# Re-ordering the steps of VectorE, ScalarE, GpSimd and the transfers of a hybrid attention layer, with TensorE's order and every address kept

## The chip, the core and the metric

The kernel runs on one core of a Trainium2 chip. TensorE (PE) does the matrix products into PSUM, which has eight banks; VectorE (DVE), ScalarE (ACT) and GpSimd (POOL) work beside it, and nearly all transfers are issued from SyncE's queue (SP). Each engine executes its own instructions strictly in the order in which they were written; engines wait for one another by semaphores. The metric is the device time of one execution in microseconds (us).

## What is computed

One decoder layer on a sequence of 512 rows of width 1024, in float32. The reference, cut to its skeleton:

```python
h = rms_norm(x, attn_pre_norm[l])
mix = hybrid_mixer(h, ...)          # one input projection, two head groups, one output projection
x = x + rms_norm(mix, attn_post_norm[l])
h = rms_norm(x, ffn_pre_norm[l])
f = (silu(h @ w_gate[l]) * (h @ w_up[l])) @ w_down[l]
x = x + rms_norm(f, ffn_post_norm[l])
```

The mixer has a differential attention of 4 heads (steps whose names begin with D) and a sparse attention of 8 heads with compressed, selected and sliding-window branches (steps that begin with N). With 512 rows every block is selected, so the selected and the window branch come down to causal attention.

## The kernel before

**Precision.** A float32 operand is cut into a high part (a rounding copy, on ScalarE mostly) and a low part (the difference, on VectorE mostly). A product is then three fast TensorE products: high by high, low by high, high by low. That is why almost every TensorE step has a ScalarE step and a VectorE step ahead of it.

**Stages in time, by the profile.** Up to about 140 us: input projection (`F`), compression and rotation of heads. From 140 to 245 us: the attention heads, with scores, row maxima (`L1051`, DVE), exponentials (`L1055`, ACT), multiplication by gates and row sums (`L1224`, POOL), transposes (`L1072`, PE), cutting of the transposed parts (`L1082` on ACT, `L1085` on DVE) and the products with the values. From 245 to 295: output projection, norms, transposes. From 295 to 505: the gate and up products of the feed-forward part, written as a seven-product scheme of 2x2 blocks (`block`, L1582). For each of 22 column blocks f there are two weight loads (`load_ff`), differences of weights (`sum_ff`, DVE), the high parts (`high_ff`, ACT) and low parts (`low_ff`, DVE at L1576), seven products of 12 matmuls each, and the evacuation of PSUM: `snap_1` and `snap_2` (ACT) copy a bank between two products, `sum_x` (DVE, L1610) and `sums` (DVE, L1626) add, `gate_x` and `gate_c` (ACT) apply silu, `mult` (DVE, L1632) multiplies. From 500 to 586: the down product in a similar scheme, with loads `load_d` and `load_22`, weight differences `sums_a` (DVE, L1682 to L1688), low parts `low_d` (L1720), `left_a` (L1699) and `right_a` (L1708), and products `product_a`, `product_b` (L1665); then the last columns (`down`, L1814) and the final norm and rows (`last_sum` to `last_row`, L1836 to L1871).

**What sets the order.** The builder defines named steps (`op`, `at`) and then calls them in the order of three lists: `PLAN` for everything up to the output projection, `PLAN_NORM` for the norms and the feed-forward part, and `PLAN_END` for its end; steps of the feed-forward part in neither of the last two lists stand between them by a planner's due time (the first argument of `at`). A step issues its instructions on its engine when it is called. So the order of the names in the lists is the order of the work on each engine and on SP's queue. A step such as `pair_sums.6.4` issues a VectorE instruction and also one or two spills to DRAM from SP's queue.

**Memory.** Every tile has a fixed place. Tags with several buffers (`raw`, `hi`, `lo`, the eight PSUM banks `b`, and others) rotate in the order of the calls; the wide buffers of the two big pools are given by tables of letters (`S_HOMES`, `HOMES`). A step that writes a place must wait until the last reader of the place's earlier tile is done: `block.18.4` accumulates into a PSUM bank that `sums.18` has to read first; `load_d.2` overwrites the weights that `low_d.0` reads; `load_22.1` those that `sums_a.0.0` and `sums_a.0.2` read. Two engines that use one PSUM bank are kept apart as well.

Of the kernel before, what the change touches and what calls it, by code (L numbers as in the profile page):

```python
# [46 lines left out]
wu xL1 gc bL1.0 xH1 xl1 bL1.1 bh1.0 F0.0.1 bl1.0 F0.1.1 F0.2.1 bh1.1 bl1.1 F2.0.1 bL1.2 bh1.2 F2.1.1 bl1.2 F2.2.1  # L47
F1.0.1 F1.1.1 F1.2.1 xS1 bL2.0 F4.0.1 F4.2.1 bh2.0 bl2.0 F4.1.1 F3.0.1 F5.2.1 F3.1.1 F3.2.1 F5.0.1 F5.1.1 xL2 xH2
F4.0.2 bL3.0 F2.0.2 F0.0.2 F0.1.2 xl2 F1.0.2 F5.1.2 bh3.0 bl3.0 xL3 xH3 F2.1.2 F2.2.2 F5.0.2 F3.0.2 F0.2.2 xl3
F1.1.2 F4.0.3 F5.2.2 F4.1.2 F3.1.2 F0.0.3 F4.2.2 xL0 xS2 xH0 F4.1.3 F3.2.2 xl0 F5.2.3 F5.0.3 F1.2.2 F5.1.3 F1.0.3  # L50
F1.1.3 F1.2.3 xS3 xA3 bL0.0 bh0.0 bl0.0 F5.2.0 F4.0.0 F4.2.3 F5.0.0 F2.0.3 xS0 F1.0.0 xL4 xH4 xl4 F2.1.3 F2.2.3
bL4.0 bh4.0 xA2 F0.1.3 F0.2.3 F5.2.4 F2.0.0 F2.1.0 F2.2.0 bl4.0 F5.1.4 xL7 xH7 F5.1.0 F0.0.0 F0.1.0 xL5 xH5 xS4 xl7
xS7 xl5 xS5 F3.0.3 cL F4.1.4 F3.1.3 F3.2.3 F3.0.0 F3.1.0 F3.2.0 F5.0.4 xL6 xH6 bL5.0 cc lL bh5.0 xl6 xA4 F1.1.0 Lv00
F4.2.4 F2.0.4 F2.1.4 F4.2.0 F4.2.5 F3.0.4 F3.1.4 xA5 F1.2.0 F3.2.4 F1.0.4 F1.1.4 xS6 xA6 F5.2.5 xA7 xA1 F0.2.0 bl5.0
# [2092 lines left out]
```

## Time and profile before

| | |
|---|---|
| median of 3 runs | 622.14 us (621.75 to 622.27) |
| the profiled execution | 622.45 us, of which its span is 620.5 us |
| moved by transfers | 98.41 MB, mean 159 GB/s |

The profile shows one execution. "Busy" is the time in which an engine had at least one instruction at work; matmuls are pipelined, so a busy TensorE may still start its matmuls more slowly than it could. Behind a row in square brackets stands how long the engine was idle before it, and whose signal ended that. "PEclk" is the TensorE clock that was granted, as a share of full speed.

### The profile page before, as it was taken

How to read it: one execution, taken by the hardware profiler on the slowest of the kernel's cores; microseconds unless marked ns; L12 is line 12 of the kernel's file. 1: busy time of each engine (PE TensorE's matmuls, PEld its weight loads, DVE VectorE, ACT ScalarE, POOL GpSimd, SP SyncE). 2: the span in 40 equal slices, each digit the busy share in tenths (PEclk: the TensorE clock that was granted, in tenths of full speed). 3: DMA queues.
4: the chain of work that ended last, by engine and by line, in shares of the span. 5: the costliest groups of instructions: out<-in, count | busy, mean ns of one | idle time of the engine just before them, and what ended most of it. 6: DMA issues, size and time to landing. Idle time of an engine off the chain costs nothing. (4 is left out here: it accounts for less than half of the span.)

```text
span 620.5 us, 10992 instructions
## 1 busy us (share of the span) xinstructions
PE 607.1 (98%) x4065; PEld 549.9 (89%) x4065; DVE 546.4 (88%) x965; ACT 373.9 (60%) x784; POOL 101.4 (16%) x153
## 2 busy tenths in 40 slices
PE   9999999999999999999999999999999799999995
PEld 5888888899999988889999999999999788878884
DVE  5898898997898884999999998899999699899977
ACT  6445375467999986577584565446464365577522
POOL 0030000307868878100000000000000000000000
PEclk9999999999999999999999999999999989999998
DMA  8566986646233211545143434353531554677413
GB/s 263 187 224 248 299 296 230 216 146 248 101 119 101 88 34 63 182 165 203 59 146 104 156 117 136 119 178 121 175 102 54 174 165 140 201 222 252 135 41 130
DMA packets 38341, 98.41 MB, mean 159 GB/s; under 512 B 4240, under 2 KB 11792, under 8 KB 37392
## 3 DMA queue, kind: packets, MB, share of 16 engines
q1 hardware_dynamic: 38144, 97.59, 47.3%
q8 instruction: 32, 0.52, 0.3%
q14 instruction: 21, 0.17, 0.1%
q10 hardware_dynamic: 144, 0.13, 0.1%
HBM read 82.10 MB, written 15.60 MB: 157 GB/s over the span
## 5 line engine op out<-in xcount | busy, mean ns | idle before, releaser
L1867 POOL TENSOR_TENSOR uf<-c,gain 128x512 f32<-128x512 f32 x1 | 1.3, 1277 | 360.1 <-DVE c L1836 360.1
L1055 ACT ACTIVATE p<-sc,nm 128x512 f32<-128x512 f32 (+3 forms) x96 | 50.2, 530 | 14.4 <-DVE nm L1051 12.9
L1051 DVE TENSOR_REDUCE nm<-sc 128x1 f32<-128x384 f32 (+3 forms) x96 | 43.4, 483 | 8.6 <-PE sc L1047 5.5
L1591 PE MATMUL yz<-rope,wbh 128*128 128x256 f32 x352 | 48.0, 280 | 0.0
L1224 POOL TENSOR_TENSOR p<-p,l 128x256 f32<-128x256 f32 (+3 forms) x64 | 45.3, 732 | 1.0
L1591 PEld LDWEIGHTS yz<-rope,wbh 128*128 128x128 f32 x352 | 44.1, 191 | 0.1
L1085 DVE TENSOR_TENSOR ptl<-tr,pth 128x384 fp32r<-128x384 f32 (+1 forms) x60 | 34.3, 592 | 8.4 <-ACT pth L1082 8.4
L1082 ACT ACTIVATE pth<-tr 128x384 fp32r<-128x384 f32 (+1 forms) x60 | 29.9, 530 | 7.3 <-PE tr L1072 6.8
L1568 ACT ACTIVATE whi<-wraw 128x1024 fp32r<-128x1024 f32 x22 | 23.2, 1057 | 13.3 <-DMA wraw<-in_wg 12.5
L1568 ACT ACTIVATE wbh<-wraw 128x1024 fp32r<-128x1024 f32 x22 | 23.3, 1057 | 12.6 <-DVE wraw L1555 7.7
L1576 DVE TENSOR_TENSOR wel<-e,weh 128x1024 fp32r<-128x1024 f32 x22 | 26.7, 1219 | 3.9 <-ACT weh L1568 2.6
L1568 ACT ACTIVATE weh<-e 128x1024 fp32r<-128x1024 f32 x22 | 23.2, 1056 | 8.0 <-DVE e L1550 6.9
L1072 PE MATMUL tr<-ident,p 128*128 128x128 f32 x200 | 27.8, 274 | 0.0
L1714 ACT ACTIVATE whi<-wraw 128x1024 fp32r<-128x1024 f32 x20 | 21.0, 1057 | 10.9 <-PE acc L1665 5.7
L1591 PE MATMUL yz<-rope,wbl 128*128 128x256 f32 x176 | 27.2, 276 | 0.0
L1576 DVE TENSOR_TENSOR wlo<-wraw,whi 128x1024 fp32r<-128x1024 f32 x22 | 26.8, 1217 | 0.0
L1576 DVE TENSOR_TENSOR wbl<-wraw,wbh 128x1024 fp32r<-128x1024 f32 x22 | 26.7, 1217 | 0.0
L1720 DVE TENSOR_TENSOR wlo<-wraw,whi 128x1024 fp32r<-128x1024 f32 x20 | 24.1, 1218 | 1.1 <-ACT whi L1714 1.1
L1621 ACT ACTIVATE us<-yz 128x512 f32<-128x512 f32 x22 | 13.0, 592 | 18.7 <-PE yz L1591 15.7
L1591 PEld LDWEIGHTS yz<-rope,wbl 128*128 128x128 f32 x176 | 23.4, 188 | 0.0
L1041 PE MATMUL sc<-kst,qst 128*128 128x384 f32 (+3 forms) x64 | 23.0, 367 | 0.3 <-DMA kst<-qk 0.3
L1072 PEld LDWEIGHTS tr<-ident,p 128*128 128x128 f32 x200 | 22.4, 141 | 0.7
(382 smaller groups left out, 1993.9 us busy)
## 6 DMA issues: line engine op xcount, KB each, us to landing
wraw<-in_wg SPq DMA_DIRECT2D x24, 512.0 KB, 3.7
wraw<-in_wu SPq DMA_DIRECT2D x22, 512.0 KB, 3.4
wraw<-in_wd SPq DMA_DIRECT2D x22, 512.0 KB, 3.7
qk<-rope SPq DMA_DIRECT2D x7, 1024.0 KB, 5.9
kst<-qk SPq DMA_DIRECT2D x24, 256.0 KB, 4.2
wraw<-in_wf SPq DMA_DIRECT2D x10, 512.0 KB, 4.2
wraw<-in_wo SPq DMA_DIRECT2D x8, 512.0 KB, 4.4
qst<-qk SPq DMA_DIRECT2D x16, 256.0 KB, 2.7
```

Source lines behind the costliest of these rows:

```text
L1041: pe.matmul(sv[i], lhs, kk[:, 0, :w], start=(n == 0), stop=False, skip_group_check=True)
L1051: dve.tensor_reduce(nm[i], sv[i], AX.X, OP.max, negate=True)
L1055: act.activation(pp[i], sv[i], AF.Exp, bias=nm[i], accum_out=hs["l"][:, row, i:i + 1])
L1072: pe.transpose(tr[:, n * P:(n + 1) * P], pp[i][:, j * P:(j + 1) * P], ident)
L1082: act.activation(part(u, 0), tv[u], AF.Copy)
L1085: dve.tensor_tensor(part(u, 1), tv[u], f32(part(u, 0)), OP.subtract)
L1224: pool.tensor_tensor(p, p, hs["l"][:, 1 + br, i:i + 1].to_broadcast(list(p.shape)), OP.mult)
L1568: act.activation(t[0], w[src], AF.Copy)
L1576: dve.tensor_tensor(t[1], W[f][PARTS[n][0]], f32(t[0]), OP.subtract)
L1591: pe.matmul(o, W[f][w][wi][:, k * P:(k + 1) * P], hop[h][hi][:, k * HS:(k + 1) * HS], start=(n < 3 and m == 0), stop=(m == 11), skip_group ...
L1714: act.activation(hi, oa[f]["raw"], AF.Copy)
L1720: dve.tensor_tensor(lo, o["raw"], f32(o["w"][0]), OP.subtract)
```

## The change

The three lists are replaced by two, `PLAN` and `PLAN_NORM`, which name the same 2585 steps in another order; `PLAN_END` and the sorting by due time go. TensorE's 800 steps stand in the same order as before. Of VectorE's 858 steps 726 stand at another position of VectorE's own order, of ScalarE's 623 steps 517, of GpSimd's 132 steps 120, of the 215 steps that use SP's queue 148; most move by a few positions, a few dozen by 15 to 76.

The places are now written behind each name (`load_d.2:0` is the first of three `raw` buffers), and a small class hands them out:

```diff
+class Spots:
+    def __init__(self, pool, tags, turn):
+        self.pool, self.tags, self.turn = pool, tags, turn
...
+    def tile(self, shape, dt, tag=None, name=None, bufs=1):
+        if tag in self.tags:
+            return self.pool.tile(shape, dt, tag=f"{tag}.{next(self.turn[0])}", name=name, bufs=1)
...
+    def run(plan):
+        for step in plan:
+            name, _, spots = step.partition(":")
+            turn[0] = iter(spots)
+            ops[name]()
...
-    plan, end = PLAN_NORM.split(), PLAN_END.split()
-    plan += [tok for _, tok in sorted(todo, key=lambda x: x[0]) if tok not in set(plan + end)] + end
...
+    plan = PLAN_NORM.split()
+    run(plan)
```

Set side by side, each letter behind a name stands for the address (or the PSUM bank) that the tile had before, and the tiles follow one another at each address in the same order as before. So what each step has to wait for is the same; what stands ahead of it in its engine's queue is not. In some 18 places two engines' uses of one PSUM bank come in the opposite order.

The places that the prediction looks at, by VectorE's, ScalarE's, GpSimd's and SP's own orders:

- **Before `sums.18` (VectorE).** Before: `low_ff.19.d sums_a.1.0 pair_sums.6.4 pair_sums.7.4 mult.17 sums_a.1.1 sum_x.20 right_a.1.1.1 sums_a.1.2 low_ff.21.d low_d.2 sums.18 low_ff.18.d`. After: `low_ff.19.d pair_sums.6.2 low_ff.21.b pair_sums.7.2 pair_sums.6.4 pair_sums.7.4 sums_a.1.0 sums_a.1.1 mult.17 sums_a.1.2 right_a.1.1.1 sum_x.20 pair_sums.6.3 low_ff.21.d sums.18 low_d.2 low_ff.18.d`. (`pair_sums.6.2`, `low_ff.21.b` and `pair_sums.7.2` stood ahead of `low_ff.19.d` before.)
- **SP there.** Before: `load_s4.1 load_22.1 load_d.2 pair_sums.6.4 pair_sums.7.4`. After: `load_d.2 load_22.1 pair_sums.6.4 pair_sums.7.4`, with `load_s4.1` ten places later.
- **ScalarE there.** `snap_2.20` now stands behind `left_a.0.1.0`, `right_a.1.1.0` and `high_d.2`; it stood ahead of all three.
- **`low_ff.16.a` (VectorE)** has seven steps fewer ahead of it: `pair_sums.3.2`, `pair_sums.3.4`, `sum_ff.16.3`, `sum_ff.16.2`, `sum_ff.16.4`, `low_ff.15.b`, `sums.12`.
- **`sums.20` (VectorE)** has three more: `pair_sums.5.3`, `left_a.0.1.1`, `left_a.2.1.1`.
- **`right_a.8.1.1` (VectorE)** has six more (`mult.20`, `cut_b.3.2.1`, `cut_b.2.2.1`, `pair_sums.8.4`, `cut_act.18.1`, `cut_b.1.2.1`) and two fewer (`sums_a.8.2`, `right_a.7.0.1`).
- **`N4L02` (VectorE, L1085)** has five more: `N5CS`, `D3X00`, `N6CX`, `N5R0`, `N5R1`.
- **`D2N4` (GpSimd)** has `N5M03`, `N5M01`, `N5M00`, `W7a` more and `W2a` fewer.
- **The end (VectorE).** `last_mean.1.1` goes ahead of `last_gain.1.0`, and the last three rows come as two halves and then the whole one instead of the whole one first.

More of the change, by code (lines that the diff above doesn't have):

```diff
@@ L172 @@
-block.17.7 high_ff.17.d low_ff.17.d gate_c.16 sum_x.18 load_ff.20.g low_ff.14.d high_ff.20.a pair_sums.2.3
-left_a.2.1.0 snap_2.18 block.18.3 block.18.7 load_ff.20.u sum_ff.20.1 sum_ff.20.2 sum_ff.20.3 high_ff.20.b
-sum_ff.20.4 pair_sums.6.1 low_ff.20.a block.20.1 high_ff.19.e low_ff.19.e pair_sums.3.3 low_ff.15.d block.19.1
-block.19.5 high_ff.20.e load_ff.21.g high_ff.21.a sums.14 low_ff.20.e block.15.4 load_ff.21.u sum_ff.21.1
-sum_ff.21.2 low_ff.21.a snap_1.19 sum_ff.21.4 pair_sums.6.2 block.19.6 mult.16 block.14.4 low_ff.20.b snap_2.19
@@ L177 @@
-block.19.3 high_ff.21.e low_ff.21.e gate_c.14 sum_x.15 gate_x.15 mult.14 sum_x.17 block.21.1 high_ff.21.d
-sum_ff.21.3 gate_c.15 mult.15 block.21.5 snap_1.21 load_22.0 snap_1.20 load_d.0 sums_a.0.0 right_a.0.1.0 sums_a.0.1
-sums_a.0.2 block.19.7 sums.19 block.20.2 block.21.6 sums.17 block.17.4 right_a.0.1.1 high_d.0 low_d.0 pair_sums.7.1
-pair_sums.6.3 load_s4.1 left_a.0.0.0 load_22.1 left_a.0.0.1 right_a.0.0.0 left_a.2.0.0 pair_sums.7.2 snap_2.21
-block.20.6 high_ff.21.b low_ff.21.b block.19.2 high_ff.19.d low_ff.19.d load_d.2 sums_a.1.0 pair_sums.6.4
@@ L182 @@
-pair_sums.7.4 gate_c.17 gate_x.17 mult.17 block.20.5 snap_2.20 high_ff.20.d block.21.2 sums_a.1.1 sum_x.20 load_d.4
-right_a.1.1.0 right_a.1.1.1 sums_a.1.2 high_d.2 low_ff.21.d low_d.2 high_ff.18.d sums.18 low_ff.18.d block.19.4
-block.21.7 load_22.2 load_d.6 sums_a.2.0 right_a.2.1.0 gate_c.19 block.21.3 sums.21 sums_a.2.1 block.20.3 sums_a.2.2
-left_a.6.0.0 right_a.2.1.1 block.18.4 gate_c.18 block.20.7 product_a.0.5 block.21.4 low_ff.20.d sums.20 block.20.4
-left_a.0.1.0 high_d.4 low_d.4 load_22.3 gate_c.21 cut_b.3.2.0 left_a.5.0.0 left_a.0.1.1 product_a.0.7 left_a.2.1.1
@@ L187 @@
-pair_sums.8.1 pair_sums.8.3 sum_x.21 sums_a.3.0 left_a.1.1.0 left_a.1.1.1 product_a.0.1 product_a.1.1 load_b.1
-left_a.4.1.0 load_b.3 product_a.1.7 product_a.2.7 sums_a.3.1 high_d.6 gate_c.20 pair_sums.8.2 load_s4.3 left_a.2.0.1
-load_s4.2 left_a.1.0.0 product_a.2.1 load_d.8 sums_a.3.2 right_a.3.0.0 low_d.6 right_a.1.0.0 cut_b.7.2.0
-right_a.0.0.1 right_a.3.1.0 right_a.3.0.1 pair_sums.7.3 right_a.3.1.1 left_a.3.1.0 left_a.1.0.1 sum_x.19
-right_a.1.0.1 load_22.4 sums_a.4.0 product_a.0.6 product_a.1.6 left_a.3.0.0 left_a.3.0.1 sums_a.4.1 sums_a.4.2
@@ L197 @@
-left_a.5.1.1 product_a.5.1 sums_a.6.0 sums_a.6.1 sums_a.6.2 product_a.4.7 product_a.5.7 right_a.6.1.0 load_d.14
-right_a.6.1.1 left_a.6.0.1 cut_b.5.1.0 high_d.12 low_d.12 load_s4.0 cut_b.0.2.0 cut_b.0.2.1 load_22.7 right_a.5.0.1
-sums_a.7.0 left_a.7.0.0 cut_b.4.2.0 sums_a.7.1 load_b.2 right_a.6.0.0 right_a.6.0.1 load_d.16 sums_a.7.2
-product_a.5.6 right_a.7.1.0 right_a.7.1.1 product_a.6.5 left_a.6.1.0 left_a.6.1.1 cut_b.2.2.0 high_d.14 low_d.14
-left_a.7.1.1 gate_x.18 product_a.6.1 mult.18 gate_x.19 load_b.7 left_a.7.0.1 cut_act.18.0 left_a.8.1.1 product_a.6.7
@@ new lines @@
+sum_ff.14.1:b sum_ff.14.2 block.12.7 snap_2.11:7 sum_ff.14.3 high_ff.14.a:21 sum_ff.14.4:m sum_x.11:2 block.11.3
+low_ff.14.a mult.5 low_ff.13.e high_ff.14.b:jg load_ff.15.u:2 high_ff.12.d:wx low_ff.14.b load_ff.15.g:1 block.13.1:2
+block.13.5 snap_1.13:5 low_ff.10.d block.12.3 sums.9:0 block.11.7 block.13.6 sum_x.12:i sum_x.10:g block.9.4
+high_ff.13.b:hc high_ff.14.e:fd pair_sums.0.3 pair_sums.2.1:9 low_ff.13.b sum_ff.15.1:a high_ff.15.a:02 sum_ff.15.2
+block.14.1:4 snap_2.13:z block.13.7 pair_sums.2.2 pair_sums.3.1:f sum_ff.15.4:a low_ff.15.a block.13.2:5 pair_sums.2.4:3
@@ new lines @@
+block.15.7 low_ff.17.b high_ff.16.d:vu low_ff.16.d gate_x.13 high_ff.17.e:hj block.15.3 low_ff.17.e sums.16:t
+block.17.1:2 block.12.4 high_ff.18.b:be snap_1.17:l high_ff.18.e:fc low_ff.18.b high_ff.15.d:zv pair_sums.1.3
+load_ff.19.g:0 block.17.5 low_ff.18.e gate_c.12 load_ff.19.u:1 block.17.6 sum_x.14:j block.18.1:0 block.16.4 gate_x.16
+snap_1.18:q high_ff.19.a:21 sum_ff.19.1:d sums.15:n mult.12 load_ff.20.g:2 mult.13 snap_2.17:d high_ff.20.a:10
+block.18.2:6 sum_ff.19.2 sum_ff.19.3 sum_ff.19.4:x high_ff.17.d:uw high_ff.19.b:ha low_ff.19.a block.18.6 sum_x.18:8
@@ new lines @@
+gate_x.18 sums.14:q low_ff.15.d gate_c.16 low_ff.19.b block.18.5 block.17.3 low_ff.17.d low_ff.20.a load_ff.20.u:0
+block.17.7 load_ff.21.g:1 snap_2.18:5 block.18.3 sum_ff.20.1:c sum_ff.20.2 high_ff.19.e:ig block.18.7 sum_ff.20.4:7
+sum_ff.20.3 low_ff.19.e low_ff.14.d block.20.1:1 block.19.1:6 block.19.5 block.15.4 high_ff.20.e:bd high_ff.20.b:jc
+high_ff.21.a:02 load_ff.21.u:2 mult.16 low_ff.20.e low_ff.21.a pair_sums.4.3 snap_1.19:a sum_ff.21.1:e block.19.6
+low_ff.20.b left_a.2.1.0:f0 snap_2.19:t sum_x.15:v block.14.4 gate_c.15 gate_c.14 sum_ff.21.2 load_d.0:0 sum_x.17:6
@@ new lines @@
+gate_x.15 pair_sums.5.3 gate_x.14 sum_ff.21.4:0 high_ff.21.e:gi snap_1.20:y low_ff.21.e block.19.3 block.21.1:4
+pair_sums.6.1:m gate_x.17 load_22.0:1 block.21.5 block.19.7 high_ff.21.d:rz left_a.0.0.0:h9 mult.15 sums_a.0.0
+sums_a.0.1 sums_a.0.2:2 mult.14 snap_1.21:l right_a.0.1.0:ea sum_ff.21.3 block.20.2:7 block.21.6 high_d.0:1 sums.17:z
+block.17.4 gate_c.17 pair_sums.7.1:d high_ff.21.b:gi low_d.0:0 sums.19:q right_a.0.1.1 block.20.6 load_d.2:0
+high_ff.19.d:ut left_a.0.0.1 snap_2.21:n low_ff.19.d pair_sums.6.2 load_22.1:1 low_ff.21.b block.19.2:5 pair_sums.7.2
@@ new lines @@
+block.20.5 block.21.2:3 pair_sums.6.4:x pair_sums.7.4 sums_a.1.0 left_a.2.0.0 sums_a.1.1 left_a.0.1.0 mult.17
+right_a.1.1.0:db high_d.2:2 snap_2.20:4 sums_a.1.2 block.19.4 right_a.1.1.1 block.21.7 sum_x.20:x high_ff.20.d:st
+load_d.4:2 pair_sums.6.3 high_ff.18.d:yv low_ff.21.d load_22.2:1 sums.18:0 low_d.2:1 load_d.6:0 block.21.3 right_a.0.0.0
+block.20.3 low_ff.18.d sums.21:2 block.18.4 sums_a.2.0 block.20.7 left_a.0.1.1 product_a.0.5:27 right_a.2.1.0:1i
+gate_c.19:5 left_a.2.1.1 gate_c.18 right_a.1.0.0 sums_a.2.1 low_ff.20.d high_d.4:0 sums_a.2.2:g block.21.4 gate_x.20
@@ new lines @@
+right_a.2.1.1 sums.20:v pair_sums.8.1:p load_s4.2:7 gate_c.21:r low_d.4:2 load_22.3:1 load_d.8:2 pair_sums.8.2
+block.20.4 left_a.1.1.0:34 product_a.0.7:60 left_a.1.0.0 pair_sums.8.3 load_s4.1:w sum_x.21 product_a.0.1:43 load_b.3:4
+left_a.1.1.1 product_a.1.1 gate_c.20 product_a.1.7 sums_a.3.0 sums_a.3.1 high_d.6:1 sums_a.3.2 mult.20 right_a.3.0.0:cj
+left_a.5.0.0:61 low_d.6:0 left_a.1.0.1 left_a.2.0.1 right_a.3.1.0 right_a.0.0.1 product_a.2.7 right_a.1.0.1
+right_a.2.0.0 sum_x.19 load_22.4:0 product_a.2.1 right_a.3.1.1 left_a.4.1.0:74 left_a.6.0.0:85 product_a.0.6:15
@@ new lines @@
+left_a.5.1.0 mult.18 left_a.3.1.0:59 pair_sums.7.3 product_a.1.6 product_a.1.5 sums_a.4.0 left_a.4.0.0 sums_a.4.1
+right_a.4.1.0:ea sums_a.4.2:h left_a.3.0.0 right_a.4.1.1 load_s4.3:z left_a.3.0.1 product_a.2.5 load_d.10:1 left_a.3.1.1
+right_a.4.0.0 right_a.3.0.1 high_d.8:2 low_d.8:1 cut_b.3.2.0:n load_22.5:0 right_a.2.0.1 product_a.3.5 sums_a.5.0
+left_a.4.0.1 sums_a.5.1 right_a.5.1.0:bd right_a.5.1.1 load_s4.0:f load_b.0:t cut_b.2.2.0:9 high_d.10:0 product_a.3.7
+load_b.1:u left_a.6.1.0 load_d.12:2 sums_a.5.2 product_a.3.1 product_a.2.6 right_a.4.0.1 product_a.3.6 low_d.10:2
@@ L413, in hybrid_block_kernel @@
     cpool.tile([P, 16], F32, name="cpad")
-    wpool = ctx.enter_context(tc.tile_pool(name="weights", bufs=3))
+    turn = [None]
+    wpool = Spots(ctx.enter_context(tc.tile_pool(name="weights", bufs=1)), ("raw", "hi", "lo"), turn)
+    for tag in ("raw", "hi", "lo"):
+        wpool.first(tag, "012", [P, 1024])
     zpool = ctx.enter_context(tc.tile_pool(name="edge", bufs=1, side="right"))
```

539 lines of the change are left out of this document (196 added, 343 removed).

## The prediction

> **What bounds the kernel now.** The page first: the busy shares.
>
> ```profile
> span 620.5 us, 10992 instructions
> PE 607.1 (98%) x4065; PEld 549.9 (89%) x4065; DVE 546.4 (88%) x965; ACT 373.9 (60%) x784; POOL 101.4 (16%) x153
> PEclk9999999999999999999999999999999989999998
> ```
>
> TensorE is busy 98% of the span and its order stays, so only the time in which it stands still or runs slowly can be won. The view of waits on TensorE, whole, says where it stands:
>
> ```profile
> PE yz L1591 <- DVE vs L1626: 3.4, 1, 3.4
> PE warm L543 <- DVE warm L540: 1.2, 1, 1.2
> PE yz L1591 <- DVE wlo L1576: 0.5, 1, 0.5
> PE sc L1041 <- DMA kst<-qk: 0.3, 1, 0.3
> PE fm L691 <- DVE wlo L684: 0.3, 1, 0.3
> ```
>
> One wait holds more than half of it. Busy time in windows around it (PE, PEld, DVE, ACT, POOL, then the granted clock, DMA share, GB/s), with two tight stages for comparison:
>
> ```profile
> 140.00:245.00 105.00, 104.65 (x776) 96.72 (x775) 85.53 (x211) 88.35 (x267) 84.53 (x131) 1.00 0.31 107
> 320.00:484.00 164.00, 163.49 (x1438) 163.22 (x1437) 155.07 (x225) 88.97 (x144) 0.00 (x0) 1.00 0.39 125
> 484.00:492.00 8.00, 8.00 (x73) 8.00 (x72) 3.24 (x7) 2.82 (x4) 0.00 (x0) 1.00 0.65 218
> 492.00:496.20 4.20, 0.78 (x7) 0.62 (x7) 4.20 (x7) 0.63 (x1) 0.00 (x0) 1.00 0.37 136
> 496.20:500.00 3.80, 3.80 (x21) 3.80 (x21) 3.77 (x7) 2.83 (x6) 0.00 (x0) 0.55 0.41 138
> ```
>
> The wait has a second part that the busy time hides: after it, from 496.2 to 500, the clock is 0.55, so 45% of 3.8 us, 1.7 us, are lost although TensorE counts as busy. And VectorE, which TensorE waits for at 492, had idled just before: 3.24 busy of 8. Its own rows, then SP's issues, then TensorE's:
>
> ```profile
> 479.96 1.22 DVE L1720 TENSOR_TENSOR wlo<-wraw,whi 128x1024 fp32r<-128x1024 f32 x1
> 483.84 0.68 DVE L1576 TENSOR_TENSOR dl<-d,dh 128x512 fp32r<-128x512 f32 x1
> 488.25 0.69 DVE L1682 TENSOR_TENSOR wraw<-wraw 128x512 f32<-128x512 f32 x1 [3.73 <-DMA wraw<-in_wd]
> 491.85 0.43 DVE L1610 TENSOR_TENSOR act<-x,snap 128x256 f32<-128x256 f32 x1 [1.03 <-DMA s<-s]
> 492.19 0.68 DVE L1708 TENSOR_TENSOR tl<-wraw,th 128x512 fp32r<-128x512 f32 x1
> 493.99 1.22 DVE L1720 TENSOR_TENSOR wlo<-wraw,whi 128x1024 fp32r<-128x1024 f32 x1
> 495.13 0.68 DVE L1626 TENSOR_TENSOR vs<-yz,us 128x512 f32<-128x512 f32 x1
> 495.73 0.68 DVE L1576 TENSOR_TENSOR dl<-d,dh 128x512 fp32r<-128x512 f32 x1
> ```
> ```profile
> 481.69 0.33 SPq L1756 DMA_DIRECT2D s4b<-s  x1
> 482.58 0.38 SPq L421 DMA_DIRECT2D wraw<-in_wd  x1
> 489.64 0.32 SPq L1658 DMA_DIRECT2D s<-s  x1
> ```
> ```profile
> 491.02 1.07 PE L1591 MATMUL yz<-rope,wbh 128*128 128x256 f32 x8
> 491.92 0.62 PE L1591 MATMUL yz<-rope,wbl 128*128 128x256 f32 x4
> 495.96 0.74 PE L1591 MATMUL yz<-x22h,dh 128*128 128x256 f32 x4 [3.42 <-DVE vs L1626]
> 503.20 0.63 PE L1591 MATMUL yz<-x22h,dh 128*128 128x256 f32 x4
> ```
>
> Read from below: `block.18.4` (495.96) waits for `sums.18` (495.13). That stood in VectorE's queue behind `sums_a.1.0` (488.25), which waited 3.73 us for the weights `load_d.2` (issued at 482.58, landed 5.6 us later), and behind `sum_x.20` (491.85), which waited 1.03 us for the spill of `pair_sums.7.4` (issued at 489.64) to free its place. `sums.18` itself needs neither: it is a wait at the head of an in-order queue.
>
> **The change, part by part.** All instructions and addresses stay; each term is a wait that goes or comes.
>
> *The wait at 492.* Eight matmuls begin at 491.02 and the next four at 491.92, 0.113 us for each, so TensorE could have started `block.18.4` at 492.4; it started at 495.96: 3.5 us. How early is `sums.18` after? Take the pitch at which VectorE's starts follow one another when it does not wait: 0.60 for 512 columns (495.13 to 495.73), 1.14 for 1024 (493.99 to 495.13), about 0.34 for 256 (491.85 to the next start at 492.19). VectorE was through with `low_ff.19.d` and all ahead of it at 484.5. After, 0.7 net comes in front of `sums_a.1.0` (`pair_sums.5.3`, `6.4`, `7.4` come, `6.3` goes), so VectorE reaches it at 485.2. Its weights: `load_d.2` waits for `low_d.0` (479.96, done at 481.2), which has two steps of 0.60 fewer and 0.34 net more ahead of it and so ends 0.9 earlier, at 480.3; it no longer stands behind `load_s4.1` (481.69); and with the present 5.6 us from issue to landing is there at 485.9. From there to the end of `sums.18` are five pitches of 0.60 (`sums_a.1.0`, `1.1`, `mult.17`, `right_a.1.1.1`, `low_ff.21.d`), 0.69 (`sums_a.1.2`), two of 0.34 (`sum_x.20`, `pair_sums.6.3`) and its own 0.68: 5.0, so 490.9. That is 1.5 before 492.4. `sum_x.20` doesn't wait again, since `pair_sums.7.4` now comes ahead of `sums_a.1.0` and its spill has 4 us. `low_ff.18.d` ends at 490.9 + 1.2 + 0.6 = 492.7; it is needed only by the third group of `block.18.4`, at 493.3. What is late next: `snap_2.20` on ScalarE now stands behind `high_d.2`, which needs `sums_a.1.1` (ends about 487.2); with 1.06 for `high_d.2` and 0.60 for itself it ends near 489, and `block.20.3` needs it at 491.0. So the cover of 1.5 us holds. If the load lands as late as now (488.2), `sums.18` ends 5.0 later, at 493.2, and TensorE waits 0.8. Value taken: **-3.5**, bounds -3.5 and -2.7.
>
> *The slow clock behind it.* The clock was 1.00 until the stop and 0.55 after it; among the 40 slices of the page's clock row only this place and the end stand below 9. If the stop goes, **-1.7** goes with it. The Trainium skill's page "TensorE: Matmul & The Clock Gate", section "What's actually happening", says that TensorE falls to half its clock after an idle window of about 3.4 us and needs about as long a busy one to return; this case agrees (0.55 for 3.8 us after 3.42 idle). By that rule a rest of 0.8 would cost no clock, and any new stop above 3.4 would cost another 1.7.
>
> *`low_ff.16.a` at 423.*
>
> ```profile
> 423.38 1.22 DVE L1576 TENSOR_TENSOR wlo<-wraw,whi 128x1024 fp32r<-128x1024 f32 x1
> 423.52 0.62 PE L1591 MATMUL yz<-x11l,whi 128*128 128x256 f32 x4
> 424.64 0.74 PE L1591 MATMUL yz<-x11h,wlo 128*128 128x256 f32 x4 [0.51 <-DVE wlo L1576]
> ```
>
> TensorE was ready at 423.52 + 4 x 0.113 = 423.97 and started at 424.64: 0.7. Seven steps of VectorE go from ahead of `low_ff.16.a`, over 4 us; the row at 423.38 has no idle time before it, so it was that queue, and not its operand, that held it. **-0.7.**
>
> *`sums.20`, three steps more ahead of it.*
>
> ```profile
> 500.58 0.69 DVE L1626 TENSOR_TENSOR vs<-yz,us 128x512 f32<-128x512 f32 x1 [0.38 <-PE yz L1591]
> 502.32 1.28 DVE L1699 TENSOR_TENSOR sl<-act,sh 128x512 fp32r<-128x512 f32 x2
> ```
>
> `left_a.0.1.1` and `left_a.2.1.1` (the two at 502.32) move ahead of it. From `low_ff.18.d` (start 492.1) nine pitches of 0.60 to 0.61 follow to its start (itself, `sums.21`, three `sums_a`, two `left_a`, `low_ff.20.d`, `right_a.2.1.1`): 497.5, end 498.2. TensorE wants it for `block.20.4` at 503.20 - 3.5 - 1.7 = 498.0. **+0.2**; bounds 0 and 1.5 (the whole of the added pitches).
>
> *`right_a.8.1.1`.*
>
> ```profile
> 542.41 0.69 DVE L1682 TENSOR_TENSOR wraw<-wraw 128x512 f32<-128x512 f32 x1 [1.68 <-issue]
> 546.15 0.68 DVE L1708 TENSOR_TENSOR tl<-wraw,th 128x512 fp32r<-128x512 f32 x1
> 546.89 0.50 PE L1665 MATMUL acc<-tl,sh 128*128 128x512 f32 x1
> ```
>
> TensorE starts this group the moment the row at 546.15 is done, so nothing is spare. Added: two steps of 0.60 and four of 0.34, minus two of 0.60, so 1.4 us; against it stands VectorE's idle 1.68 ahead of it, which shrinks as loads move with the rest. TensorE wants it 5 us earlier, VectorE arrives about 4.3 to 4.8 earlier. **+0.3**; bounds 0 and 2.1 (the 1.4 and the 0.7).
>
> *The attention stage.* Here four engines are over 80% busy (first window), and nearly every step moves. The tightest:
>
> ```profile
> 202.34 0.56 DVE L1085 TENSOR_TENSOR ptl<-tr,pth 128x384 fp32r<-128x384 f32 x1
> 203.67 0.42 PE L1041 MATMUL sc<-kst,qst 128*128 128x384 f32 x1
> 209.24 0.20 POOL L1155 TENSOR_TENSOR dr<-dr 128x4 f32<-128x4 f32 x1 [1.74 <-ACT dr L1179]
> ```
>
> `N4L02` (202.34) is read out 0.8 before TensorE overwrites its bank (203.67), and five small steps, 1.6 us of VectorE, come ahead of it: bounds 0 and 0.8; VectorE idles 19% of this stage, so half, **+0.4**. `D2N4` on GpSimd (209.24) gets 2.05 us more ahead of it, but 1.74 of that was idle: nothing.
>
> *SP, and the end.* Loads that move keep the 3 to 4 us between issue and use that they have; the rows at the end change only among themselves, as many VectorE steps between the last product and the last row as before: 0, with 0.3 either way.
>
> Sum: -3.5 - 1.7 - 0.7 + 0.2 + 0.3 + 0.4 = **-5.0**. The profiled execution took 622.45 us (its span of 620.5 and 1.95 around it), so 617.4; the median of the runs, 622.14, lies 0.3 below that execution: **617.1 us**.
>
> **The rivals.**
>
> 1. *More is won.* The costs that I add (0.9) don't come, and the small waits of TensorE's list (0.3 and 0.3) go too: 617.1 - 1.5 = 615.6. Down to 614.0 for halts that the list shows too small, as the one at 424 (0.5 there, 0.7 by its starts). For it: VectorE idles 8.9 us between 320 and 484 (164.0 less 155.07), so new waits there need not reach TensorE.
>
> 2. *The gain is given back later.* From 500 to 590 VectorE must now deliver 5 us earlier. With all my upper bounds (1.5, 2.1, 0.8) and 0.8 left at 492: 622.14 - 5.1 + 4.4 = 621.4, no difference that can be told. That the order has no effect on the engines would look the same; since each engine works in order, I give that next to nothing.
>
> 3. *Slower: the banks of the attention stage.*
>
> ```profile
> DVE nm L1051 <- ACT p L1055: 2.6, 3, 1.7
> ```
>
> Between 140 and 250 us VectorE's row maximum waited three times, 0.87 us each, for ScalarE's exponential on the other part of the same PSUM bank. The new order changes which of the two comes first in some 18 such places. A wait of 0.87 is about the 0.8 that a step is ahead of TensorE there (203.67 against 202.90), so each further wait goes through nearly whole, once VectorE's lead is used up. The Trainium skill's page "PSUM — Partial Sum Buffer", section "PSUM bank collisions raise a hardware error", says that two engines must not be at one bank at once, reads included; so such a wait can't be dropped. From 8 waits on (5.0 that is won and 1.2 that can be told, by 0.87) the kernel is slower than before; with ten it is 617.1 + 8.7 = 625.8. Against it: only three such waits show now, and TensorE shows one wait of 0.3 in the whole stage.
>
> **How the numbers follow.** A difference of 0.2%, 1.2 us, is about what a measurement of this kernel can tell from no change. My forecast (616 to 620.9) gets 0.50, rival 1 (below 616) 0.18, rival 2 (620.9 to 623.4) 0.15, rival 3 0.17. So faster 0.68, same 0.15, slower 0.17. The range leaves out rival 3 and a little of rival 1: 614.0 to 622.8.
>
> **What would show it.** Right: no idle of TensorE at 492 and a clock of 1.00 in the slices around 500; `sums_a.1.0` waiting under 1.5 us; no `[0.51` row near 424. Wrong: a wait of TensorE for DVE `vs` L1626 or ACT `snap` L1601 around 490 to 498; new waits for DVE `tl` or `sl` between 540 and 560; a wait list with several rows of `sc` L1041 or `tr` L1072 for rival 3; a second stretch of low clock. The forecast fails above all if VectorE stops at another head of its queue, for a load that the new order uses sooner than it lands.

## The result, and the profile after

| | before | after |
|---|---|---|
| median of the runs | 622.20 us | 628.98 us (627.47 to 630.31) |
| profiled execution (span) | 622.45 us (620.5) | 630.31 us (628.5) |
| ratio to before | | 1.0104, 95% interval 1.0073 to 1.0136 |

The kernel became 6.8 us slower. The forecast was 617.1 us in a range of 614.0 to 622.8, with a chance of 0.17 for slower: the time lies outside the range, 6.2 us above its upper end.

The page of after, its span, busy shares and granted clock:

```profile
span 628.5 us, 10996 instructions
...
PE 611.1 (97%) x4065; PEld 549.0 (87%) x4065; DVE 554.7 (88%) x965; ACT 373.8 (59%) x784; POOL 104.6 (17%) x153
...
PEclk9999999998999999999999999999999999999999
```

VectorE executes the same 965 instructions as before, and is busy for 554.7 us in place of 546.4; GpSimd's 153 take 104.6 in place of 101.4. Work that is only put in another order should not grow. That is the first trace of the cause, and it stands in the third line of the page.

TensorE's waits after (engine, line, what it waited for, then us in total, times, longest us):

```profile
PE warm L423 <- DVE warm L420: 1.2, 1, 1.2
PE sc L895 <- DVE ptl L965: 1.0, 1, 1.0
PE yz L1473 <- DVE wlo L1458: 0.9, 1, 0.9
PE ms L1027 <- DVE dv L724: 0.9, 1, 0.9
PE sc L921 <- DMA kst<-qk: 0.8, 1, 0.8
PE scc L1081 <- DVE rope L604: 0.8, 1, 0.8
PE yz L1473 <- DVE vs L1508: 0.7, 1, 0.7
```

The wait of 3.4 us has left the list. In its place stand many waits of 1 us and less, nearly all for VectorE (the list goes on with eleven more below 0.7).

Since TensorE's order is the same, the start of one and the same matmul in the two traces shows where the time goes. The lag is after less before:

| step | start before | start after | lag, us |
|---|---|---|---|
| F7.1 | 103.60 | 104.31 | +0.72 |
| N1SC | 122.51 | 124.30 | +1.78 |
| D0MS | 146.61 | 150.12 | +3.51 |
| N3S0 | 159.10 | 164.44 | +5.35 |
| D3S01 | 203.67 | 213.38 | +9.71 |
| N6TC | 233.96 | 244.38 | +10.42 |
| block.0.7 | 316.94 | 330.24 | +13.30 |
| block.16.2 | 425.22 | 437.87 | +12.64 |
| block.18.4 | 495.96 | 504.83 | +8.88 |
| product_a.0.5 | 500.38 | 508.09 | +7.71 |
| block.20.4 | 503.20 | 511.73 | +8.53 |
| product_a.8.1 | 547.92 | 556.13 | +8.20 |

Until 100 us there is no lag. The attention stage (100 to 235 us) costs 10.4, the norms and the first feed-forward blocks 2.9 more; then the gains come that were forecast, 0.7 at 425, 3.8 at 496, 1.2 behind it. The windows around the old wait show it gone (columns as in the prediction):

```profile
493.00:501.00 8.00, 8.00 (x73) 8.00 (x72) 7.70 (x13) 4.45 (x8) 0.00 (x0) 1.00 0.57 197
501.00:505.00 4.00, 4.00 (x38) 4.00 (x37) 3.96 (x8) 2.79 (x5) 0.00 (x0) 1.00 0.68 197
505.00:509.00 4.00, 3.78 (x28) 3.43 (x28) 3.90 (x7) 1.45 (x4) 0.00 (x0) 1.00 0.42 137
```

VectorE is busy 7.70 of 8 us ahead of it (3.24 before), and the clock is 1.00 throughout (0.55 before). Only 0.22 is left, for `low_ff.18.d`.

Which of VectorE's rows grew? The view of groups by line and shape, in the window 95 to 265 us, of before (number, busy us, mean ns of one):

```profile
L1051 DVE TENSOR_REDUCE nm<-sc 128x1 f32<-128x512 f32 x23 | 15.7, 686 | 4.0 <-PE sc L1047 3.9
...
L1121 DVE SCALAR_TENSOR_TENSOR p<-p,l 128x384 f32<-128x384 f32 x4 | 2.6, 656 | 0.0
...
L1228 DVE TENSOR_TENSOR pc<-pc,l 128x128 f32<-128x128 f32 x8 | 2.3, 291 | 0.3 <-POOL l L1220 0.3
L1213 DVE TENSOR_TENSOR pc<-pc,nmc 128x128 f32<-128x128 f32 x8 | 2.3, 282 | 0.1
...
L1121 DVE SCALAR_TENSOR_TENSOR p<-p,l 128x128 f32<-128x128 f32 x4 | 1.3, 331 | 0.0
```

and of after:

```profile
L931 DVE TENSOR_REDUCE nm<-sc 128x1 f32<-128x512 f32 x23 | 15.6, 680 | 3.1 <-PE sc L927 3.0
...
L1108 DVE TENSOR_TENSOR pc<-pc,l 128x128 f32<-128x128 f32 x8 | 6.1, 757 | 0.0
L1093 DVE TENSOR_TENSOR pc<-pc,nmc 128x128 f32<-128x128 f32 x8 | 4.0, 499 | 0.1
...
L1001 DVE SCALAR_TENSOR_TENSOR p<-p,l 128x384 f32<-128x384 f32 x4 | 3.7, 934 | 0.0
...
L1001 DVE SCALAR_TENSOR_TENSOR p<-p,l 128x128 f32<-128x128 f32 x4 | 2.4, 594 | 0.0
```

The row maximum `nm`, which reads scores from PSUM, takes 0.68 us in both. The products `p<-p,l` (the steps `D0MX0` to `D3MX3`) and `pc<-pc,l` (`N0CM` to `N7CM`), whose inputs both lie in SBUF, grow up to 2.6 times. One of them, `N4CM`, on VectorE's timeline and GpSimd's rows at the same moment (start, us):

```profile
205.36 1.17 DVE L1108 TENSOR_TENSOR pc<-pc,l 128x128 f32<-128x128 f32 x1
...
204.41 1.98 POOL L1104 TENSOR_TENSOR p<-p,l 128x256 f32<-128x256 f32 x3
```

GpSimd's three rows run until 206.39 (204.41 + 1.98); the VectorE row ends at 206.53 and took 1.17 us. The same step in before:

```profile
199.89 0.28 DVE L1228 TENSOR_TENSOR pc<-pc,l 128x128 f32<-128x128 f32 x1
...
200.70 0.73 POOL L1238 TENSOR_TENSOR pcs<-pc,pcs 128x256 fp32r<-128x256 f32 x1 [1.40 <-ACT pcs L1236]
```

GpSimd had been waiting for 1.40 us, until 200.70, and the row took 0.28.

Taken over all traces of this study, a VectorE step's surplus is its length above the shortest that the same step shows in any of them, where that is over 0.15 us. After has 24 such rows with 12.8 us; before has 3 with 2.4. This gives the theory to be tested, called **P** below: where a VectorE row with two SBUF inputs and a GpSimd row that reads SBUF meet, the later one stands until the earlier is through, and VectorE, which was busy for 81% of this stage before (85.53 of 105 us), passes most of it on to TensorE.

### The profile page after: what moved, and what is told of

Same layout as the page of the kernel before. It is cut to its first block, busy times and chain, and to the rows that moved or that the text cites. A ratio compares the mean times of both kernels' runs of the same rounds, so it can differ in the third digit from the quotient of the medians.

```text
span 628.5 us, 10996 instructions
## 1 busy us (share of the span) xinstructions
PE 611.1 (97%) x4065; PEld 549.0 (87%) x4065; DVE 554.7 (88%) x965; ACT 373.8 (59%) x784; POOL 104.6 (17%) x153
## 4 chain that ended last, share of the span: by engine, by line
PE 71%; DVE 17%; DMA 4%; ACT 3%; issue 3%; SPq 1%; DVEq 0%; POOL 0%; ACTq 0%; POOLq 0%
PE yz L1473 26%; PE acc L1547 14%; PE fm L588 5%; PE fm L571 5%; PE x L1473 3%; PE acc L1696 3%; PE tr L952 2%; PE v L704 2%; PE avn L1135 2%; PE mixp L1206 2%; DVE nm L931 2%; DMA wraw<-in_kw 2%; PE g L704 2%; DVE p L1001 1%; PE sc L921 1%
## 5 line engine op out<-in xcount | busy, mean ns | idle before, releaser
L935 ACT ACTIVATE p<-sc,nm 128x256 f32<-128x256 f32 (+3 forms) x96 | 50.2, 532 | 17.5 <-DVE nm L931 15.2
L1104 POOL TENSOR_TENSOR p<-p,l 128x256 f32<-128x256 f32 (+3 forms) x64 | 47.5, 765 | 0.8
L921 PE MATMUL sc<-kst,qst 128*128 128x384 f32 (+3 forms) x64 | 23.6, 377 | 1.1 <-DMA kst<-qk 0.8
L922 PE MATMUL sc<-kst,qst 128*128 128x384 f32 (+3 forms) x64 | 22.2, 349 | 0.0
```

The source lines that it names most:

```text
L935: act.activation(pp[i], sv[i], AF.Exp, bias=nm[i], accum_out=hs["l"][:, row, i:i + 1])
L1104: pool.tensor_tensor(p, p, hs["l"][:, 1 + br, i:i + 1].to_broadcast(list(p.shape)), OP.mult)
```

## The experiments

In all of them the addresses are those of the two kernels and TensorE's order is kept; only queues of the other engines change, except where it is said. Ratios are to before, run beside them.

**One: which part of the list costs.** PLAN holds the steps up to the end of attention, PLAN_NORM the rest.

```diff
 PLAN = """
-wu:00 xL1:0 bL1.0:0 bh1.0:0 bl1.0:0 gc bL1.1 bL1.2 xH1:k xl1:e bh1.1 bh1.2 F0.0.1:7 F0.1.1 F0.2.1 xL2 bl1.1 bl1.2
+wu:00 xL1:0 gc bL1.0:0 xH1:k xl1:e bL1.1 bh1.0:0 F0.0.1:7 bl1.0:0 F0.1.1 F0.2.1 bh1.1 bl1.1 F2.0.1:6 bL1.2 bh1.2
...
```

> The order of before up to the end of the attention stage (PLAN), the new order from the norms on (PLAN_NORM). Theory A, the loss comes from the order of the attention stage: TensorE's lag of 10.5 us that the trace of after shows between 100 and 235 us is gone, the gains at 424 and 496 (0.7, 3.6 and 1.2 us) stay and the 3 us lost between 245 and 300 stay: 622.2 - 5.5 + 3 = 619 to 620. Theory B, the attention stage only shows a loss that has its cause elsewhere (the later stages of the new order, or a lower clock): 625 or more.

Measured: 0.9953 (0.9933 to 0.9973), 619.3 us by the ratio to 622.2. Theory A holds. Beside before, its trace loses 2.0 us between 290 and 302 and gains afterwards as after does. The other half, PLAN of after with PLAN_NORM of before:

> The new order up to the end of the attention stage, the order of before from the norms on. Theory A: the lag of 10.5 us comes and nothing is won later, 622.2 + 10.5 = 632 to 633. Theory B: 621 to 624. If the old order of the norms has slack that takes up a late attention stage, 625 to 630.

Measured: 1.0237 (1.0215 to 1.0258), 636.52 us, 4 us more than expected. Most of the expected lag of the attention stage comes (8.4 us at D3S01); the surplus over the expectation arises between 293 and 318 us, where the old order of the norms runs behind the new order of attention and loses another 4 us, part of it in 3.4 us of halved clock from 330.6 us of its own time on. Lists that were made for one another do not mix freely, as the next two show more strongly.

**Two: one pair of queues at a time**, in PLAN, with PLAN_NORM of after.

```diff
 m1: VectorE, ScalarE: order of after
-    GpSimd, SyncE:    order of after
+    GpSimd, SyncE:    order of before
```

> After, but in the attention part GpSimd and SyncE keep the order of before; VectorE and ScalarE have the new one. Rival 3 of the prediction (banks, or anything in the order of VectorE and ScalarE against each other): as after, 627 to 631. Rival theory G (GpSimd's weight splits moved among its multiplies, or loads issued at other moments, make VectorE late): 618 to 621.

> After, but in the attention part VectorE and ScalarE keep the order of before; GpSimd and SyncE have the new one. Rival 3 or another cause in the order of VectorE and ScalarE: 618 to 621. Theory G (GpSimd or the loads): 627 to 631. If each of the two pairs costs a part, both kernels lie between, 621 to 627.

Measured: m1 1.0569 (1.0538 to 1.06), m2 1.0347 (1.0328 to 1.0367). Both miss, and neither theory gave such times. The list of waits of m1 says why:

```profile
PE fm L576 <- ACT whi L566: 4.7, 2, 4.2
PE fm L576 <- DVE xl L452: 3.6, 1, 3.6
PE tr L957 <- POOL p L1109: 2.9, 3, 1.6
```

Loads in one order and their readers in another cost much ahead of attention already: at 95 us TensorE is 20.4 us late in m1, and 12.4 in m2. The two runs say nothing about which pair is at fault.

**Three: a seam in time.** The list of before up to TensorE's step at a given time, then what is left in the order of after.

```diff
-PLAN = steps of after
+PLAN = steps of before ahead of TensorE's step at 108 us (h1) or 160 us (h2), the others in the order of after
```

> The order of before for all that it lists ahead of TensorE's work at 108 us, the new order for the rest. Theory P: in the new order VectorE and GpSimd run beside one another at other places, and there the same VectorE instructions take longer (1.17 us in place of 0.28 for the row pc<-pc,l of N4CM, while GpSimd's 1.04 us multiply ran); in all the trace of after has 23 such places and 12.6 us, before 3 and 2.4 us, and VectorE has no time to spare there. Nearly all of them lie after 108 us, so the loss comes back but for the 2 us that the late weight load at 98 us (KW03) costs: 618.6 of the first experiment + 7 to 8.5 = 626 to 627. Theory L, the late load at 98 us takes VectorE's lead and the rest follows from it: 619 to 620.5.

> The same with the seam at 160 us. Theory P: what lies behind 160 us stays, by TensorE's lag 10.5 - 5.3 = 5 us: 623 to 624. Theory L: 618.5 to 619.5, as without any of the new order in this stage.

Measured: h1 1.0108 (1.0072 to 1.0143), h2 1.0021 (1.0003 to 1.0039). Theory L falls: without the late load h1 is as slow as after. P holds, for h2 to the us (622.2 x 1.0021 = 623.5), for h1 with 2 us more than expected. The surplus of VectorE's rows is 11.9 us in h1 and 9.5 in h2. Most of those 2 us of h1 go with a stretch of halved clock that its trace shares with that of after (1.6 us by its lag there, see the last section): the one of its five executions with a mean granted clock of 0.998 took 626.98 us, as expected, and the four with 0.994 and 0.995 took 629.06 to 631.02.

**Four: little on GpSimd that VectorE could meet.** GpSimd's multiplies of the sparse heads' probabilities are left out and its splits of `wo` replaced by memsets.

```diff
-            pool.tensor_tensor(p, p, hs["l"][:, 1 + br, i:i + 1].to_broadcast(list(p.shape)), OP.mult)
+            pass
...
-            to_r(eng[0], hl[0][c], get()[:, c * SEQ:(c + 1) * SEQ])
+            pool.memset(f32(hl[0][c]), 0.0)
```

> After, without GpSimd's multiplies of the sparse heads' probabilities by gate and 1/sum, and with GpSimd's splits of wo replaced by memsets (both left out, so the output is another one); the steps of the other engines and their order are as in after. Theory P: with little left on GpSimd that VectorE can meet, VectorE's 10 us go, 629 - (7 to 10) = 619 to 622. If it is the order of VectorE's and ScalarE's queues itself, or the banks: 626 to 629.

> The same left out of before, as a control of how much the removal itself is worth. Theory P: before has 2.4 us of longer instructions, at two places one of which is the attention stage's, so 620.5 to 622. If the removal helps by freeing waits and not by meetings, before gains as much as after, several us.

Measured: a2 0.9971 (0.9952 to 0.9991), that is 8.3 us below after by the ratios (1.0104 less 0.9971, of 622.2); b2 1.0004 (0.9982 to 1.0026), nothing. So the removal is worth nothing by itself, and 8.3 us where VectorE met this work. The groups of a2 in the window 95 to 265 us, with the queues of VectorE and ScalarE as in after:

```profile
L1001 DVE SCALAR_TENSOR_TENSOR p<-p,l 128x384 f32<-128x384 f32 x4 | 2.4, 605 | 0.0
L1107 DVE TENSOR_TENSOR pc<-pc,l 128x128 f32<-128x128 f32 x8 | 2.3, 282 | 0.0
...
L1001 DVE SCALAR_TENSOR_TENSOR p<-p,l 128x128 f32<-128x128 f32 x4 | 1.4, 344 | 0.0
```

934 ns became 605 again, and 757 became 282. TensorE's lag at D3S01 is 1.9 us in place of 9.7. The trace holds a finer point. `D2MX0` and `D2MX1`, the rows `p<-p,l` x2, in after with GpSimd's rows beside them:

```profile
189.43 2.25 DVE L1001 SCALAR_TENSOR_TENSOR p<-p,l 128x128 f32<-128x128 f32 x2
...
189.07 1.29 POOL L1158 TENSOR_TENSOR ol<-opair,oh 128x512 fp32r<-128x512 f32 x1
190.30 1.10 POOL L315 CAST whi<-wraw 128x1024 fp32r<-128x1024 f32 x1
```

and in a2:

```profile
184.70 0.74 DVE L1001 SCALAR_TENSOR_TENSOR p<-p,l 128x128 f32<-128x128 f32 x2
...
184.71 0.95 POOL L1241 MEMSET whi<- 128x1024 f32 x1
```

The subtraction and the cast, which read SBUF, hold them; a memset, which only writes, stands beside them at no cost.

**Five: a dose, and its reverse.** Two splits of GpSimd go ahead in before (d1), and six are moved away in after (f1). GpSimd's queue alone changes:

```diff
 d1
-D2g N3g1 N3M11 W5h W5l N3M12
+D2g W5h W5l N3g1 N3M11 N3M12
 f1
-W3b W3d W3a N0g0
+N0g0
...
-N0M13 D1g
+N0M13 W3b W3d W3a D1g
...
-N1OL W1h W6b W1l N3g1 N3M13 N3M12 N3M11 N3M10 W5h
+N1OL N3g1 N3M13 N3M12 N3M11 N3M10 W1h W1l W5h
...
-N4PL D1N4
+N4PL W6b D1N4
```

> Before, with one move on GpSimd: the two steps W5h and W5l (1.04 and 2.4 us) go ahead of N3g1 and N3M11, so that they run beside VectorE's D2MX0, D2MX1 and D2MX3. No queue of another engine changes. Theory P: these rows, 0.34, 0.48 and 0.74 us, take up to 1 us more each, 1 to 2 us in all, and TensorE loses 1 to 1.8 us between 185 and 200 us: 1.0016 to 1.003 of before. If the lengths of VectorE's rows do not hang on GpSimd, or VectorE has room there: no change of any row, ratio 1.000.

> After, with six of GpSimd's splits of wo moved on its own queue to where VectorE's rows read from PSUM or GpSimd stands still (W3b, W3d, W3a behind N0M13; W1h, W1l behind N3M10; W6b behind N4PL); the other queues as in after. Theory P: of the 12.7 us the parts beside D0MX2, D0MX3, gl0 and D2MX1 to D2MX3 go, 2.9 us, if no new meetings come: 626 to 627.5. If meetings do not matter: 629, or later where the multiplies come later.

Measured: d1 1.0034 (1.0019 to 1.0049), 2.1 us, a little above the range; f1 1.0038 (1.0018 to 1.0058), 624.6 by the ratio, 4.1 us below after where 1.5 to 3 were expected. In d1 `D2MX1` (0.47 us before) stood for 2.69 beside `W5l`, and `D2MX0` (0.34 before) for 1.12 beside `W5h`. d1's view of the line `p<-p,l` (number, then the shortest, median and longest ns), its timeline of GpSimd, and its list of TensorE's waits:

```profile
L1006 DVE SCALAR_TENSOR_TENSOR p<-p,l x16: 302/616/2689, 112.6 to 225.7; 128x512 f32<-128x512 f32 x4, 128x384 f32<-128x384 f32 x4, 128x128 f32<-128x128 f32 x4, 128x256 f32<-128x256 f32 x4
```
```profile
184.08 2.39 POOL L1250 TENSOR_TENSOR wlo<-wraw,whi 128x1024 fp32r<-128x1024 f32 x1
```
```profile
PE sc L926 <- ACT p L940: 1.4, 1, 1.4
```

The length added to `D2MX1`, 2.2 us, is nearly W5l's 2.39. TensorE has a new wait of 1.4, and its lag grows by 2.4 us between 180 and 189: two GpSimd steps on the wrong side of two VectorE steps. In f1 the surplus of VectorE's rows falls by 2.9 us only, so the rest of its 4.1 has another source; the halved clock of the trace of after (last section) is not in f1's.

**Six: both on one engine.** Two rows of GpSimd cannot meet.

```diff
-            dve.tensor_tensor(cv, cv, hs["l"][:, 0].unsqueeze(2).to_broadcast([P, NT, NPAD]), OP.mult)
+            pool.tensor_tensor(cv, cv, hs["l"][:, 0].unsqueeze(2).to_broadcast([P, NT, NPAD]), OP.mult)
```

> After, with the eight products pc<-pc,l (128x128, 6.1 us with 3.9 us of lengthening in after) on GpSimd in place of VectorE, at the same places of the list. Theory P: VectorE gets 6 us back, 3.9 of them by meetings; TensorE's lag falls by 3 to 5 us: 624 to 626. Rival: GpSimd is over 80% busy from 155 us on, and 3 to 4 us more there make its multiplies late: TensorE waits for GpSimd's p rows (tr L952), 628 to 632.

Measured: 1.0063 (1.0038 to 1.0087), 626.1 by the ratio, 2.6 us below after where P gave 3 to 5; TensorE waits for GpSimd's `p` rows for 0.2 us only.

**Seven: a version that beats both.**

```diff
-PLAN, PLAN_NORM = steps of after
+PLAN, PLAN_NORM = steps of before ahead of TensorE's step at 303 us, the others in the order of after
```

> The order of before for all that it lists ahead of TensorE's work at 303 us, the new order from there. Against the first experiment (0.9953 of before) this also keeps the old order of the norms and of the first feed-forward blocks, where that kernel lost 2.15 us between 290 and 302 us: 622.2 x 0.9953 - 2.15 = 617.1, 0.992 of before. If the later gains need what the new order does at 290 to 302 us (loads or buffers made ready there): 618.5 to 620.

Measured: 0.9916 (0.9892 to 0.994), 617.0 by the ratio. The gains of the change stay and its costs go. The 2.0 us of the norms lay in the order of that stretch: with its old order TensorE's lag stays at 1.3 us from 290 to 302. The ratio alone would not show that, since the interval of e3 meets that of e1. The profiled execution of this kernel held a surprise. VectorE and GpSimd in e3, then in before, in the same order:

```profile
185.93 2.96 DVE L1006 SCALAR_TENSOR_TENSOR p<-p,l 128x512 f32<-128x512 f32 x1
...
185.96 2.38 POOL L1250 TENSOR_TENSOR wlo<-wraw,whi 128x1024 fp32r<-128x1024 f32 x1
```
```profile
186.39 0.74 DVE L1121 SCALAR_TENSOR_TENSOR p<-p,l 128x512 f32<-128x512 f32 x1
...
186.43 2.96 POOL L1365 TENSOR_TENSOR wlo<-wraw,whi 128x1024 fp32r<-128x1024 f32 x1
```

The two start 0.03 to 0.04 us apart in both. In before GpSimd stands (2.96 in place of 2.38), in e3 VectorE does (2.96 in place of 0.74), and TensorE loses 1.6 us at 189. The last two kernels move `D2MX3` to where GpSimd must wait for a later VectorE step.

```diff
-D2MX2 D2MX0 D2MX1 N3R1 v1d2 N2L12 N4X11 N4X01 N4X02 D2MX3 N4X03
+D2MX2 D2MX0 D2MX1 D2MX3 N3R1 v1d2 N2L12 N4X11 N4X01 N4X02 N4X03
```

> The kernel of e3 with one VectorE step moved: D2MX3 goes from behind N4X02 to right behind D2MX1. There GpSimd stands still, since its next step N3g1 needs VectorE's N3R1, which now comes behind D2MX3. In the trace of before D2MX3 began 0.04 us ahead of GpSimd's W5l (2.4 us) and took 0.74; in the trace of e3, with the same order, it took 2.9 and TensorE lost 1.6 us at 189. Theory P, the one that starts first holds the other for its whole length, so it was chance: 0.74 in the trace, no loss at 189, and the runs near 620 to 621 no longer come; median 0.3 to 1.2 us below e3, 0.987 to 0.991 of before. If e3's long row was something else: as e3, 0.9916, with the same spread.

> Before with the same single move. Theory P: D2MX3 takes 0.74 us in every run, so at most the 1.6 us go, in those runs that lost them: 0.997 to 1.000 of before. If the move costs what is queued behind D2MX3 (0.74 us for N3R1 to N4X02, which have 0.9 to 2.3 us to spare): up to 1.001.

Measured: e4 0.9935 (0.9923 to 0.9947), b4 1.000 (0.9986 to 1.0015). In both traces `D2MX3` takes 0.74 to 0.75 us and TensorE loses nothing at 189. e4's executions lie between 618.05 and 618.86 us, e3's between 616.44 and 621.05. But the median did not fall, and e4 cannot be told from e3, whose interval meets its own. So the place is mended, as P says, but how often the meeting went wrong there, and how much of the spread of before it makes, stays open.

## Why the prediction was wrong

**The step that failed** is the term "The attention stage", which said "bounds 0 and 0.8; VectorE idles 19% of this stage, so half, **+0.4**". It measured 10.4 us by TensorE's lag at N6TC. The term looked at one tight hand-over, `N4L02` ahead of `D3S01`, and took the durations of rows as fixed while "nearly every step moves". They are not: a row's length held only for the GpSimd row that happened to stand beside it in before. The rows of after are 12.8 us longer in 24 places; in a2, where three such rows with 1.9 us are left, the lag at D3S01 falls from 9.7 to 1.9, the 1.9 being new hand-overs (D3S01 itself, and 0.8 at F7.1 behind a late load). So about 8 of the 10 us came with the meetings, some 1.5 of them by way of a halved clock behind one of the waits that they made (last section), and some 2 us were what the term meant to price. The same holds for its last sentence on GpSimd, `D2N4`, "2.05 us more ahead of it, but 1.74 of that was idle: nothing": `D2N4` itself cost nothing, but GpSimd's queue was weighed by lateness, and never by what runs beside it.

The trace of before could have shown it. Its groups hold the sister rows of one shape:

```profile
L728 DVE TENSOR_TENSOR rope<-rope 128x512 f32<-128x512 f32 x3 | 3.1, 1047 | 0.0
L729 DVE TENSOR_TENSOR rope<-rope 128x512 f32<-128x512 f32 x3 | 2.0, 681 | 0.0
```

Same operation and shape, 1047 against 681 ns: one of the three, `pA3` at 115.72, took 1.78 us beside a GpSimd split. The mean of a group that is above its sister's is the mark to look for. Before has only three such rows among hundreds. Whether its order had been arranged around them is not shown; that a change of nearly every step lost this is what after shows.

The Trainium skill states the mechanism. Its page "SBUF — State Buffer", section "SBUF: two separate sides", says that VectorE and GpSimd share one pair of SBUF ports, taken as an exclusive lock for a whole instruction, and that a VectorE operation with two SBUF inputs needs it against a GpSimd operation that reads SBUF. The traces agree: `nm<-sc` and `ptl<-tr`, with one input in PSUM, began while a GpSimd row was at work in 104 of 152 cases between 100 and 265 us in after, and none was over 0.15 us longer; of the rows `p<-p,l`, 8 of the 11 beside GpSimd were longer; memsets held nothing. Which of the two goes first can't be read from the starts where these are 0.01 to 0.04 us apart: in d1 and e3 the VectorE row with the earlier start was the one that stood.

**Rival 3** had the sign, the stage and about the time (625.8, and 629.0 came), but another mechanism: ten waits of VectorE's row maximum for ScalarE on a PSUM bank. That wait, in before and in after, by VectorE's list:

```profile
DVE nm L1051 <- ACT p L1055: 2.6, 3, 1.7
```
```profile
DVE nm L931 <- ACT p L935: 0.2, 1, 0.2
```

It shrank. (The three waits of before were not 0.87 us each, as the prediction has it: that is their mean, and one of them was 1.7.) Rival 3 as written did not happen; that its time came near is luck.

**The other terms, by TensorE's lag.** The wait at 492: -3.5 forecast, -3.76 measured. `sums.18` ended 0.5 us ahead of its use, not 1.5, and `low_ff.18.d` was 0.22 late. The slow clock: -1.7 forecast, -1.2 measured; its price was not as fixed as the term took it (last section). `low_ff.16.a`: -0.7, and -0.66. `sums.20`: +0.2 forecast, +0.8 measured, inside its bounds of 0 and 1.5; the row that it delays is the one named (`block.20.4`, waiting 0.68 for `vs`). `right_a.8.1.1`: +0.3 forecast, -0.3 measured, just below its lower bound. SP and the end: the lag is 8.2 us from there to the last matmul and 8.1 at the end of the last row, so 0 holds within its 0.3. The norms and the first feed-forward blocks had no term at all and cost 2.9 us between 235 and 317; the one meeting among the rows of the norms has its like in before (`U1.0` lost 1.0 us beside `N7OL`, and in before `U3.0` lost 1.1 beside the same step). By e1 and e3 some 2 us lie in the order of that stretch, which was not taken apart further.

Summed up: the part of the list on which most of the working was spent went nearly as forecast. Its terms add up to -5.4 without the attention stage, TensorE's lag falls by 5.1 from 317 us to the end, and e3 shows this part alone (4.7 by its lag there, 617.0 us by the ratio). The list contained a second, larger change, priced with half of one row.

## What to carry to other kernels

Before pricing a re-ordering, list the rows of VectorE whose inputs both lie in SBUF and lay GpSimd's timeline beside them, in the old order and in the new: each meeting can cost up to nearly the whole of the other row (2.2 us in d1), and in a stage where VectorE is nearly full it reaches TensorE. If an engine's busy total grows while its count of instructions stays, compare groups of one shape by their mean before looking at waits. And where two such rows start within some hundredths of a us, tie their order by a dependency instead of leaving it to the execution, as e4 and b4 do; a gain in time from this could not be told there.

## What the runs showed of the hardware

GpSimd loses as well as VectorE: `W5l` took 2.96 us in before, where `D2MX3` beside it kept its 0.74, and 2.38 in e3, where `D2MX3` stood. The one that waits can do so for nearly the whole of the other: `D2MX1`, 0.47 us long, for 2.2 of the 2.39 of `W5l` in d1.

The granted clock halved in the profiled execution of after at a place where TensorE had waited for 0.87 us only (busy columns, then the clock, as above):

```profile
148.00:150.30 2.30, 1.43 (x13) 1.30 (x12) 2.30 (x4) 2.30 (x10) 2.30 (x2) 1.00 0.00 0
150.30:152.20 1.90, 1.90 (x14) 1.90 (x15) 1.82 (x6) 0.70 (x4) 0.27 (x1) 0.68 0.92 362
152.20:154.30 2.10, 2.10 (x6) 1.62 (x6) 1.81 (x5) 0.60 (x1) 0.00 (x0) 0.50 1.00 228
```

In the trace of before the one such stretch ahead of the end stood behind a wait of 3.42 us. So the prediction's sentence that a rest of 0.8 would cost no clock does not hold for this execution. The stretch lasts from 151.0 to 154.4 us; h1's trace has one from 150.7 to 154.1, behind a wait of 0.86. In e2, with the same order and the same wait of 0.86 us there, the clock stayed at 1.00 and TensorE was 1.5 us earlier behind it. The executions of after seem to differ in the same way: two have a mean granted clock of 0.995 and took 629.84 and 630.31 us, two have 0.998 and 0.999 and took 628.11 and 627.47, and 3.4 us at half the clock are 0.003 of the mean. What decides this was not tried; about 1.5 of the 8 us between the two profiled executions is this.

Nor was the length of such a stretch fixed. Behind the wait at 492 of the old order it was 3.4 us in the trace of before, and 6.8 us in those of d1, b2 and b4, where TensorE's lag grows by 0.8 to 0.9 us between 496 and 500.
